# Small fp32 products of a two-layer kernel regrouped by array halves and column groups, bias rows made in one product at the head, other room for scan parameters

## The chip, the cores and the metric

One core of a Trainium2 chip runs the program. The number is the device time of one execution in microseconds; lower is better. TensorE (PE) has a granted clock of 1.2 or 2.4 GHz; the profile gives it as a share of the higher level.

## The reference

`x` is 1024 tokens by 1024 channels, fp32, and passes through two layers.

```python
# layer 1
h = rmsnorm(x, norm_mix_pre);  q, k, v, u, g_attn, g_ssm = split(h @ w_in)
# attention, 8 heads of 64 on 2 key/value heads, blocks of 128 queries on the block's own and the previous 128 keys
logits = q @ k.T / 8 + rel_bias[bucket(qpos - kpos)]          # masked to a window of 128
m = max(logits, sink);  p = exp(logits - m);  probs = p / (sum(p) + exp(sink - m))
y_attn = (probs @ v) @ w_attn_branch
# scan: 32 groups of 16 channels, one complex diagonal state of 64 each
s_t = a * s_(t-1) + B u_t;  y_t = Re(C s_t) + d_skip * u_t;  z = gelu(y);  z = z * sigmoid(z @ w_glu)
merged = sigmoid(g_attn) * y_attn + sigmoid(g_ssm) * (z @ w_ssm_branch)
x = x + rmsnorm(merged @ w_out);  x = x + rmsnorm(relu(rmsnorm(x) @ w_ff_in)**2 @ w_ff_out)
# layer 2: a gated, a convolution and a pooling branch on one big projection, and a last rmsnorm (not touched)
```

## The kernel before

The big products split each fp32 operand into a high and a low fp16 part and add three products (L208, L209, L210 in `pair_products`), and Strassen's scheme makes seven products of half size out of eight. One such product moves 512 columns. The weights come by SyncE DMAs into `raw`, a pool of three 512 KB buffers (`load_k`, L145), are subtracted on DVE (`tw`, L164) and split by ACT (`whi`, L135) and DVE (`wlo`, L136). The small products are made in fp32, which takes two passes, so two records, for each product; a transpose takes one.

The program is a list of units (`do`); each may have a `prepare` part that loads and splits its weights ahead. A scheduler then sets the order in which each engine's instructions stand, and an engine runs its own in that order; semaphores hold one until what it needs is there. So in the trace the small products of attention and scan stand between big products of other units.

**The head (L529 to L541).** Eight tiles of 128 tokens, t0 to t7, are loaded by SP. For each, ACT sums the squares (L540), POOL takes the power -0.5 (L428), DVE scales the tile (L541), PE transposes it (L448), and ACT and DVE split it. `first_pair` makes keys and values (L383): tokens 0 to 255 need t0 and t1, tokens 256 to 511 t2 and t3, the second half t4 to t7. The first queries follow in the same way.

**The bias (L573 to L592)** comes after the second half of the queries. The 32 by 8 table is copied to 128 columns for each head; eight products of 33x128x384 (L586) with a one-hot table give `vrow`, the same row in all 128 partitions; ACT copies each (L587); POOL's queue writes it to DRAM (`bdr`, L589) and reads it back so that each partition starts one element further left (`bias_t`, L591).

**Attention (L763 to L820).** `attend(n)` makes the logits of block n (L773) and the probabilities; `values(n)` transposes these (L800) and multiplies with `vtok` (L807): for each key/value head, each parity of the query head and each half of the band one product of 256 columns, that is eight in a block and four in the first. The output takes 64 of the 128 columns of the array.

**The scan (L882 to L986)** runs in four groups of eight channel groups. `ssm_tables` makes tables on DVE, 32 records of `pwk` (L921, 64 rows by 16 columns, on either half of the rows) and transposes (L934). `ssm_scan` makes `S` (L944, 32 records that alternate between the two halves of the array's columns), scans on DVE, and sums `py` from one product of `Kt` (L969, all 128 rows) and two of `CA` (L971, 64 rows) for each of eight output pieces, the three in a row.

Of the kernel before, what the change touches and what calls it, by code (L numbers as in the profile page):

```python
# [50 lines left out]
def kernel(ctx: ExitStack, tc: tile.TileContext, I: dict, out: bass.AP):  # L51
# [14 lines left out]
    def A32(kb, n):  # L66
        o = int(kb * KB) // 4
        return arena[:, o:o + n]
# [266 lines left out]
    def linear2(W, c0, act, cb, scale, early=None):  # L335
# [3 lines left out]
        def prepare():  # L339
            raw = load_k(W, lambda w: w.rearrange("(k p) n -> p k n", p=P), c0)  # L340
# [185 lines left out]
    K32 = [A32(92 + 8 * q, 4 * H).rearrange("p (k t) -> p k t", k=4) for q in range(4)]  # L526

    @do
    def _():  # L529
        xin = [A32((72, 56)[t // 4] + 4 * (t % 4), D) for t in range(NT)]  # L530
        for t in range(NT):
# [3 lines left out]
            if t == 1:  # L535
                prepare(1)
# [22 lines left out]
    bias_t = A32(84, 8 * 256).rearrange("p (h s) -> p h s", h=8)  # L559
    sink = small([P, 8], "sink")  # L560

    @do
    def _():
        nc.vector.tensor_copy(kk[0:64, 1, :], kk[64:128, 0, :])
# [7 lines left out]

    @do  # L573
    def _():

        relb = small([33, 8], "relb")
        nc.vector.memset(relb, 1.0)
        nc.gpsimd.dma_start(out=relb[0:32, :], in_=I["rel_bias"])
        hot = A32(92, 384)[0:33, :]
        nc.gpsimd.dma_start(out=hot, in_=I["onehot"])  # L580
        relrep = A32(94, 8 * P)[0:33, :].rearrange("p (h m) -> p h m", h=8)
        nc.vector.tensor_copy(relrep, relb.unsqueeze(2).to_broadcast([33, 8, P]))
        vrow = A32(108, 8 * 384).rearrange("p (h i) -> p h i", h=8)
# [6 lines left out]
        skew = bass.AP(bdr.tensor, bdr.offset + 127, [[8 * 384 - 1, P], [384, 8], [1, 256]])  # L590
        nc.gpsimd.dma_start(out=bias_t, in_=skew)  # L591
        nc.gpsimd.dma_start(out=sink, in_=I["sinks"][0].partition_broadcast(P))  # L592
# [13 lines left out]
    toff = [92.0]  # L606

    def tmp(n):
        a = A32(toff[0], n)
        toff[0] += n * 4 / KB  # L610
        assert toff[0] <= 108
        return a
# [13 lines left out]
    def _():  # L626
        L16 = tmp(3 * P)[0:16, :].rearrange("p (i m) -> p i m", i=3)
# [8 lines left out]
        prm = tmp(48).rearrange("p (i r) -> p i r", i=3)  # L636
# [3 lines left out]
        def EXP(dst, src, n):  # L640
            save = toff[0]
# [15 lines left out]
        def SINCOS(sn, cs, y, n):  # L657
            save = toff[0]
# [34 lines left out]

        dt_ = small([P, 16], "dt")
# [13 lines left out]
        TT(Ai[:, 1, :], mags[:, 0, :], snd[:, 0, :], ALU.mult)  # L708
        for m in (1, 2, 4):
# [4 lines left out]
        nr, den, f_r, f_i, t1 = (tmp(16) for _ in range(5))  # L714
# [13 lines left out]
        braw = tmp(512).rearrange("p (i r c) -> p i r c", i=2, r=NP)  # L728
# [4 lines left out]
        tb1 = tmp(256).rearrange("p (r c) -> p r c", r=NP)  # L733
        tb2 = tmp(256).rearrange("p (r c) -> p r c", r=NP)
        cmul(Bf[:, 0], Bf[:, 1], frb, fib, braw[:, 0], braw[:, 1], tb1, tb2)
        for i, n_ in enumerate(("c_re", "c_im")):
            craw = tmp(256).rearrange("p (u q) -> p u q", u=4)
# [52 lines left out]
    def values(n):  # L790
        pr = Pb[n % 2]
        for kv in range(2):
            pv = aux("pvo")
            for par in range(2):
                pt = aux("pt")
                for i in range(2):
                    h = kv * 4 + par + 2 * i
                    for half in range(2):
                        if n or half:
# [726 lines left out]
```

## Time and profile before

| what | value |
|---|---|
| median of 3 runs | 2028.05 us (2022.07 to 2031.63) |
| profiled execution | 2025.8 us, of which the span 2024.1 |
| PE busy | 1971.5 us, 97% |
| DVE busy | 1534.5 us, 76% |
| ACT busy | 875.8 us, 43% |
| POOL busy | 105.4 us, 5% |
| mean granted clock of PE | 0.994 |

The span runs from the first to the last instruction; 1.7 us of the execution lie around it. The shares are means over very different stretches: the loading of x (0 to 37 us), the first projections (to 98), attention beside big products (to about 270), the scan beside the attention gate (288 to 440) and then the rest, which the diff does not touch.

### The profile page before, as it was taken

The numbers are of one execution on the slowest core, as the hardware profiler recorded it, in microseconds if no ns is written. First come the engines' busy times: TensorE is split into PE (matmuls) and PEld (weight loads), VectorE is DVE, ScalarE is ACT, GpSimd is POOL, SyncE is SP. The second block draws the span as 40 slices with busy tenths as digits, with TensorE's granted clock in tenths as the row PEclk, the third lists the DMA queues.
The fourth block names the chain that finished last, engine by engine and source line by source line (L and its number), as shares of the span: only waits on it lengthen the run. The fifth ranks groups of instructions, "written<-read, shape, count | busy, mean of one in ns | idle before, by whom it ended". The sixth has DMA issues, their size and how long they took to land. (4 is left out here: it accounts for less than half of the span.)

```text
span 2024.1 us, 25660 instructions
## 1 busy us (share of the span) xinstructions
PE 1971.5 (97%) x9536; PEld 938.3 (46%) x9536; DVE 1534.5 (76%) x2830; ACT 875.8 (43%) x1691; POOL 105.4 (5%) x157
## 2 busy tenths in 40 slices
PE   7999999999999999999999999999999999999998
PEld 5434445554454444444444444454444443444443
DVE  7687679877568966878876578589678896899942
ACT  7316643334246735625527445434333332344511
POOL 1000000110010000000000011000000011110000
PEclk9999999999999999999999999999999999999999
DMA  5231162577321221121122422211111121112222
GB/s 182 87 109 53 42 132 69 162 235 254 104 89 63 63 73 42 63 62 53 58 68 94 126 76 86 67 43 60 63 56 62 53 63 31 63 63 68 89 84 84
DMA packets 130574, 171.80 MB, mean 85 GB/s; under 512 B 12025, under 2 KB 98293, under 8 KB 130320
## 3 DMA queue, kind: packets, MB, share of 16 engines
q1 hardware_dynamic: 124736, 160.46, 24.4%
q0 software_dynamic: 3536, 8.64, 2.4%
q10 hardware_dynamic: 2176, 1.05, 0.3%
q8 instruction: 75, 1.23, 0.2%
q14 instruction: 51, 0.42, 0.1%
HBM read 138.01 MB, written 30.93 MB: 83 GB/s over the span
## 5 line engine op out<-in xcount | busy, mean ns | idle before, releaser
L208 PE MATMUL b<-arena,whi 128*128 128x512 f16 x2044 | 776.8, 380 | 9.1 <-ACT p L226 6.5
L209 PE MATMUL b<-arena,whi 128*128 128x512 f16 x2044 | 777.2, 380 | 0.9 <-DVE arena L136 0.9
L210 PE MATMUL b<-arena,wlo 128*128 128x512 f16 x2044 | 776.5, 380 | 0.0
L135 ACT ACTIVATE whi<-tw 128x512 f16<-128x512 f32 x292 | 172.9, 622 | 337.6 <-DVE tw L164 286.8
L209 PEld LDWEIGHTS <-whi 128*128 128x128 f16 x2044 | 200.5, 98 | 253.1 <-issue 19.8
L210 PEld LDWEIGHTS <-wlo 128*128 128x128 f16 x2044 | 200.5, 98 | 243.1 <-issue 7.6
L208 PEld LDWEIGHTS <-whi 128*128 128x128 f16 x2044 | 200.5, 98 | 242.6 <-issue 8.0
L253 DVE SCALAR_TENSOR_TENSOR c<-b,u 128x512 f32<-128x512 f32 x204 | 139.7, 686 | 109.9 <-PE b L210 109.6
L136 DVE SCALAR_TENSOR_TENSOR wlo<-tw,whi 128x512 f16<-128x512 f32 x292 | 194.2, 683 | 7.7 <-ACT whi L135 7.4
L136 DVE SCALAR_TENSOR_TENSOR wlo<-raw,whi 128x512 f16<-128x512 f32 (+1 forms) x261 | 176.7, 687 | 13.9 <-ACT whi L135 13.7
L415 PEld LDWEIGHTS <-arena 128*128 128x128 f16 x1152 | 112.7, 98 | 133.2
L135 ACT ACTIVATE whi<-raw 128x512 f16<-128x512 f32 (+1 forms) x261 | 151.2, 609 | 41.5 <-PE b L209 17.0
L164 DVE TENSOR_TENSOR tw<-raw,tw 128x512 f32<-128x512 f32 x134 | 91.8, 685 | 1.4 <-DMA raw<-in_w_in_dram 0.4
L843 ACT ACTIVATE c<-c 128x512 f32<-128x512 f32 x60 | 37.7, 629 | 116.6 <-DVE c L253 98.4
L354 PE MATMUL pl<-arena,whi 128*128 128x512 f16 x320 | 83.1, 379 | 2.2 <-DVE fetch L997 1.8
L415 PE MATMUL po<-arena 128*128 128x512 f16 x384 | 84.0, 379 | 0.0
L415 PE MATMUL pf<-arena 128*128 128x512 f16 x384 | 84.0, 379 | 0.0
L415 PE MATMUL pw<-arena 128*128 128x512 f16 x384 | 83.0, 379 | 0.0
L231 DVE SCALAR_TENSOR_TENSOR u<-b,p 128x512 f32<-128x512 f32 x79 | 54.0, 684 | 33.0 <-PE b L210 32.9
L383 PE MATMUL pq<-arena,whi 128*128 128x512 f16 (+1 forms) x288 | 79.0, 360 | 0.0
L237 DVE SCALAR_TENSOR_TENSOR u<-b,u 128x512 f32<-128x512 f32 x79 | 54.1, 685 | 17.6 <-PE b L210 17.5
L226 ACT ACTIVATE p<-b 128x512 f32<-128x512 f32 x79 | 46.0, 583 | 38.2 <-PE b L210 38.2
(326 smaller groups left out, 2175.5 us busy)
## 6 DMA issues: line engine op xcount, KB each, us to landing
raw<-in_w_in_dram SPq DMA_DIRECT2D x86, 512.0 KB, 3.5
raw<-in_w_ff_in_dram SPq DMA_DIRECT2D x32, 512.0 KB, 3.6
raw<-in_w_ff_out_dram SPq DMA_DIRECT2D x32, 512.0 KB, 3.5
fetch<-gdr SPq DMA_DIRECT2D x32, 256.0 KB, 4.2
xr<-xdr SPq DMA_DIRECT2D x32, 256.0 KB, 3.4
gdr<-c SPq DMA_DIRECT2D x24, 256.0 KB, 2.0
arena<-in_x_dram SPq DMA_DIRECT2D x8, 512.0 KB, 9.9
raw<-in_w_out_dram SPq DMA_DIRECT2D x8, 512.0 KB, 5.6
```

What stands on the lines that cost most here:

```text
L135: ACT(hi, src, AF.Copy, scale=scale)
L136: STT(lo, src, scale, hi, ALU.mult, ALU.subtract)
L164: TT(t, a, b, ALU.subtract)
L208: MM(b[:, 0:n], whi[:, k], act[0][:, i, k, sl], start=(first and k == 0), stop=False, skip_group_check=not first)
L209: MM(b[:, 0:n], whi[:, k], act[1][:, i, k, sl], start=False, stop=False, skip_group_check=not first)
L210: MM(b[:, 0:n], wlo[:, k], act[0][:, i, k, sl], start=False, stop=(k == nk - 1), skip_group_check=not first)
L231: STT(v["u2"], o2, scale, v["p1"], ALU.mult, ALU.add)
L237: STT(v["u3"], o, scale, v["u2"], ALU.mult, ALU.add)
L253: STT(d, vw(o), scale, vw(v[u]), ALU.mult, ALU.add)
L354: MM(bs[s], w[:, k], a[:, k, s * H:(s + 1) * H], start=(k == 0 and w is hi and a is act[0]), stop=(k == 3 and w is lo))
L383: MM(o, w[:, k % 4], a, start=(k == 0 and w is hi and a is ahi), stop=(k == 7 and w is lo))
L415: MM(bs[s], part(a), w[:, s * H:(s + 1) * H], start=(k == 0 and a is ahi and w is whi), stop=(k == nk - 1 and a is alo))
```

## The change

- **Bias.** `bias_rows` runs while x is being loaded: one product of 33x8x384 gives the eight rows in eight partitions, ACT copies them once, and POOL's queue writes each 128 times to `bdr` (1536 KB out of 12 KB in eight partitions). `bias_read` reads it back as before, now from the unit after the first projections.
- **values.** A block has four transposes into each of four banks and four products of 512 columns, which alternate between the two halves of the array's columns; one split instead of two. The order of rows in `at` is another, so `w_attn_branch` is loaded by two DMAs of 64 partitions each (`by_kv`).
- **pwk.** The four pieces r lie in four groups of 32 columns of the array instead of side by side in the bank; four ACT copies of 16x128 stand where one of 16x512 did.
- **py.** All eight `Kt` products come first, then the sixteen `CA` products, alternating between the two halves of the array's rows and two banks.
- **Scan parameters.** Their scratch room moves from 92..108 KB, which the probabilities use later, to 131..136 and 142 onwards.

```diff
-    def linear2(W, c0, act, cb, scale, early=None):
+    def linear2(W, c0, act, cb, scale, early=None, by_kv=False):
...
+            if by_kv:
+                raw = pw.tile([P, 4, 256], F32, tag="raw", name=nm("raw"), bufs=3)
+                for a in range(2):
+                    nc.sync.dma_start(out=raw[64 * a:64 * a + 64],
+                                      in_=W[256 * a:256 * a + 256].rearrange("(k p) n -> p k n", p=64)[:, :, c0:c0 + 256])
...
+    def bias_rows():
+        relb = small([33, 8], "relb")
+        nc.vector.memset(relb, 1.0)
+        nc.gpsimd.dma_start(out=relb[0:32, :], in_=I["rel_bias"])
+        hot, row = q2("hot"), q2("vrow")
+        nc.gpsimd.dma_start(out=hot[0:33, 0:384], in_=I["onehot"])
+        pb = aux("pbias")
+        MM(pb[0:8, 0:384], relb, hot[0:33, 0:384], start=True, stop=True)
+        nc.scalar.copy(row[0:8, 0:384], pb[0:8, 0:384])
+        nc.gpsimd.dma_start(out=bdr.rearrange("p (h i) -> h p i", h=8),
+                            in_=row[0:8, 0:384].unsqueeze(1).to_broadcast([8, P, 384]))
+        nc.gpsimd.dma_start(out=sink, in_=I["sinks"][0].partition_broadcast(P))
+
+    def bias_read():
+        skew = bass.AP(bdr.tensor, bdr.offset + 127, [[8 * 384 - 1, P], [384, 8], [1, 256]])
+        nc.gpsimd.dma_start(out=bias_t, in_=skew)
...
             if t == 1:
+                bias_rows()
                 prepare(1)
...
     @do
     def _():
+        bias_read()
         nc.vector.tensor_copy(kk[0:64, 1, :], kk[64:128, 0, :])
...
-        for h in range(8):
-            pb = aux("pbias")
-            MM(pb[:, 0:384], relrep[:, h, :], hot, start=True, stop=True)
-            nc.scalar.copy(vrow[:, h, :], pb[:, 0:384])
-        bdr = pdr.tile([P, 8 * 384], F32, tag="bdr", name="bdr")
-        nc.gpsimd.dma_start(out=bdr, in_=vrow.rearrange("p h i -> p (h i)"))
...
-    toff = [92.0]
+    toff = [131.0]
...
-                for half in range(2):
-                    if n or half:
-                        MM(pv[par * 64:(par + 1) * 64, 0:256], vtok[:, n - 1 + half, kv * 64:(kv + 1) * 64],
-                           pts[:, half * 256:half * 256 + 256], start=(half == 0 or n == 0), stop=(half == 1))
...
+        parts = [(half, kv) for half in range(0 if n else 1, 2) for kv in range(2)]
+        pts = {}
+        for half, kv in parts:
+            pt = aux("pt")
+            for i in range(4):
+                nc.tensor.transpose(pt[:, i * P:(i + 1) * P], pr[:, 4 * kv + i, half * P:(half + 1) * P], ident)
+            pts[half, kv] = A32(142 + 2 * (2 * half + kv), H)
+            nc.scalar.copy(pts[half, kv], pt)
+        pv = aux("pvo")
+        for half, kv in reversed(parts):
+            MM(pv[kv * 64:(kv + 1) * 64, :], vtok[:, n - 1 + half, kv * 64:(kv + 1) * 64], pts[half, kv],
+               start=(half == 1), stop=(half == parts[0][0]))
...
+            for i in range(2):
+                for r in range(4):
+                    MM(pk[32 * r:32 * r + C, 0:P], Bf[rows, i, p0 + r, :],
+                       CA[rows, i, r, 0:8, :].rearrange("p d c -> p (d c)"), start=(i == 0), stop=(i == 1))
             for r in range(4):
-                for i in range(2):
-                    MM(pk[0:C, r * P:(r + 1) * P], Bf[rows, i, p0 + r, :],
-                       CA[rows, i, r, 0:8, :].rearrange("p d c -> p (d c)"), start=(i == 0), stop=(i == 1))
-            nc.scalar.copy(Wsb[:, :, a, :], pk[0:C, :].rearrange("p (r m) -> p r m", r=4))
+                nc.scalar.copy(Wsb[:, r, a, :], pk[32 * r:32 * r + C, 0:P])
...
+        for r in range(4):
+            for a in range(2):
+                MM(pys[a][:, cols_[r]], Kt[:, 2 * r + a, :], U[:, 2 * r + a, :], start=(r == 0), stop=False,
+                   skip_group_check=(r > 0))
+        for r in range(4):
+            for i in range(2):
+                for a in range(2):
+                    rows = slice(a * 64, (a + 1) * 64)
+                    MM(pys[a][:, cols_[r]], CA[rows, i, r, 1:9, :].rearrange("p d c -> p (d c)"), Ht[rows, i, r, :],
+                       start=False, stop=(i == 1), skip_group_check=(r > 0))
```

The scheduler gives the head another order, too. On DVE, where L541 (before) and L572 (after) scale a tile and `rs_28` (before) and `rs_32` (after) belong to t2, the rows of before are:

```order
L136 SCALAR_TENSOR_TENSOR arena<-tr_123,arena 128x4x128 [waits Activation_49]
L136 SCALAR_TENSOR_TENSOR arena<-tr_128,arena 128x4x128 [waits Activation_49]
L541 SCALAR_TENSOR_TENSOR arena<-arena,rs_24_141 128x1024 [waits DMAHW2_49,Pool_49]
L426 TENSOR_SCALAR rs_28_163<-ss_27_161 128x1 [waits DVE_49,Activation_49]
L541 SCALAR_TENSOR_TENSOR arena<-arena,rs_28_163 128x1024 [waits DMAHW5_49,Pool_49]
L136 SCALAR_TENSOR_TENSOR arena<-tr_145,arena 128x4x128 [waits Activation_49]
L136 SCALAR_TENSOR_TENSOR arena<-tr_150,arena 128x4x128 [waits Activation_49]
L426 TENSOR_SCALAR rs_32_185<-ss_31_183 128x1 [waits DVE_49]
L541 SCALAR_TENSOR_TENSOR arena<-arena,rs_32_185 128x1024 [waits DMAHW6_49,Pool_49]
```

t2 stands directly behind t1. In the changed kernel the last of the rows ahead of t2 are these (`raw_479`, `raw_648` and `raw_650` are the fourth to sixth weight loads behind those of keys and values):

```order
L136 SCALAR_TENSOR_TENSOR wlo_494<-tw_485,whi_493 128x512 [waits Activation_49]
L136 SCALAR_TENSOR_TENSOR wlo_500<-tw_497,whi_499 128x512 [waits Activation_49]
L136 SCALAR_TENSOR_TENSOR wlo_504<-raw_479,whi_503 128x512 [waits Activation_49]
L136 SCALAR_TENSOR_TENSOR wlo_510<-tw_507,whi_509 128x512 [waits Activation_49]
L136 SCALAR_TENSOR_TENSOR wlo_514<-raw_479,whi_513 128x512 [waits Activation_49]
L164 TENSOR_TENSOR tw_656<-raw_648 128x512 [waits DMAHW7_49]
L164 TENSOR_TENSOR tw_658<-raw_650,tw_656 128x512 [waits DMAHW0_49,DVE_49]
L164 TENSOR_TENSOR tw_668<-raw_650,raw_648 128x512
L164 TENSOR_TENSOR tw_678<-raw_650,tw_658 128x512 [waits DVE_49]
L572 SCALAR_TENSOR_TENSOR arena<-arena,rs_32_175 128x1024 [waits Pool_49]
L434 TENSOR_SCALAR rs_36_197<-ss_35_195 128x1 [waits DVE_49]
L572 SCALAR_TENSOR_TENSOR arena<-arena,rs_36_197 128x1024 [waits Pool_49]
```

In all 11 splits (L136) and 8 differences (L164) of six weight loads have moved ahead of t2; before, they stood behind the tiles. POOL, which issues the bias DMAs and takes the powers of the tiles, has before:

```order
L428 TENSOR_TENSOR rs_20_119<-rs_20_119,mhalf_75 128x1 [waits DVE_49]
L578 DMA relb_773<-in_rel_bias_dram 32x8
L631 DMA ldt_808<-in_log_dt_dram 16x2
L428 TENSOR_TENSOR rs_24_141<-rs_24_141,mhalf_75 128x1 [waits DVE_49,Pool_49]
L428 TENSOR_TENSOR rs_28_163<-rs_28_163,mhalf_75 128x1 [waits DVE_49,Pool_49]
L428 TENSOR_TENSOR rs_32_185<-rs_32_185,mhalf_75 128x1 [waits DVE_49,Pool_49]
L428 TENSOR_TENSOR rs_36_207<-rs_36_207,mhalf_75 128x1 [waits DVE_49,Pool_49]
L428 TENSOR_TENSOR rs_40_229<-rs_40_229,mhalf_75 128x1 [waits DVE_49,Pool_49]
L428 TENSOR_TENSOR rs_44_251<-rs_44_251,mhalf_75 128x1 [waits DVE_49,Pool_49]
L428 TENSOR_TENSOR rs_48_273<-rs_48_273,mhalf_75 128x1 [waits DVE_49,Pool_49]
L746 DMA arena<-in_d_skip_dram 16x512 [waits DMAHW1_49,DVE_49]
L580 DMA arena<-in_onehot_dram 33x384 [waits DVE_49,Activation_49]
```

And in the changed kernel:

```order
L436 TENSOR_TENSOR rs_24_131<-rs_24_131,mhalf_75 128x1 [waits DVE_49]
L641 DMA ldt_788<-in_log_dt_dram 16x2
L436 TENSOR_TENSOR rs_28_153<-rs_28_153,mhalf_75 128x1 [waits DVE_49,Pool_49]
L549 DMA bdr<-vrow_96 8x128x384 [waits Activation_49]
L436 TENSOR_TENSOR rs_32_175<-rs_32_175,mhalf_75 128x1 [waits DVE_49,Pool_49]
L436 TENSOR_TENSOR rs_36_197<-rs_36_197,mhalf_75 128x1 [waits DVE_49,Pool_49]
L556 DMA arena<-bdr 128x8x256 [waits DMASW4_49,DMAHW6_49,DVE_49,Activation_49]
L436 TENSOR_TENSOR rs_40_219<-rs_40_219,mhalf_75 128x1 [waits DVE_49,Pool_49]
L436 TENSOR_TENSOR rs_44_241<-rs_44_241,mhalf_75 128x1 [waits DVE_49,Pool_49]
L436 TENSOR_TENSOR rs_48_263<-rs_48_263,mhalf_75 128x1 [waits DVE_49,Pool_49]
L436 TENSOR_TENSOR rs_52_285<-rs_52_285,mhalf_75 128x1 [waits DVE_49,Pool_49]
L638 DMA arena<-in_lam_re_dram 16x128 [waits DMAHW1_49,DVE_49]
```

The write of `bdr` (L549) now stands ahead of t2's power, and the read (L556), which waits for the write (DMASW4), ahead of the powers of t4 to t7.

## Rows read from the trace of the kernel before

**Rows 1.** The page, busy time of the whole span (share, instructions), PE.

```profile
PE 1971.5 (97%) x9536; PEld 938.3 (46%) x9536; DVE 1534.5 (76%) x2830; ACT 875.8 (43%) x1691; POOL 105.4 (5%) x157
```

**Rows 2.** Windows: length, busy us of each engine, PEclk, DMA share, GB/s.

```profile
86.00:98.00 12.00, 12.00 (x35) 5.50 (x34) 1.50 (x3) 4.91 (x10) 1.59 (x3) 0.72 0.41 158
150.00:270.00 120.00, 119.25 (x572) 58.47 (x571) 78.94 (x279) 70.53 (x215) 5.00 (x8) 1.00 0.29 57
288.00:440.00 152.00, 150.42 (x904) 86.61 (x903) 129.43 (x242) 56.19 (x92) 19.92 (x38) 1.00 0.50 147
```

**Rows 3.** Timeline of PE, attention: start us, us, engine, line, tiles, count.

```profile
163.40 0.38 PE L208 MATMUL b<-arena,whi 128*128 128x512 f16 x1
163.71 0.65 PE L807 MATMUL pvo<-arena 128*64 128x256 f32 x2
164.29 0.66 PE L800 MATMUL pt<-ident,arena 128*128 128x128 f32 x4
...
183.11 1.08 PE L807 MATMUL pvo<-arena 128*64 128x256 f32 x4
184.12 1.13 PE L773 MATMUL lg<-arena 64*128 64x256 f32 x6
```

**Rows 4.** Timeline of PE, scan: pwk alone, and S on alternating column halves.

```profile
288.29 3.24 PE L921 MATMUL pwk<-arena 64*16 64x128 f32 x32
291.47 1.09 PE L934 MATMUL pg<-ident,arena 128*128 128x128 f32 x8
...
303.72 1.97 PE L944 MATMUL S<-arena 128*64 128x128 f32 x32
```

**Rows 5.** Timeline of PE, scan: py of one group, first rows and end.

```profile
315.99 0.38 PE L969 MATMUL py<-arena 128*128 128x128 f32 x2
316.30 1.07 PE L971 MATMUL py<-arena 64*128 64x128 f32 x4
...
324.70 0.39 PE L209 MATMUL b<-arena,whi 128*128 128x512 f16 x1
```

**Rows 6.** Timeline of PE: bias products, and the tenth big product behind them.

```profile
85.99 6.93 PE L586 MATMUL pbias<-arena 33*128 33x384 f32 x16
...
96.63 0.38 PE L208 MATMUL b<-arena,whi 128*128 128x512 f16 x1
```

**Rows 7.** Waits of DVE, 288 to 440 us: total us, times, longest.

```profile
DVE wlo L136 <- ACT whi L135: 7.3, 4, 4.2
DVE arena L949 <- PE S L944: 6.7, 4, 2.1
```

**Rows 8.** Timeline, head: DVE, ACT and PE.

```profile
9.98 1.29 DVE L136 SCALAR_TENSOR_TENSOR wlo<-raw,whi 128x512 f16<-128x512 f32 x2 [2.12 <-ACT whi L135]
...
14.82 1.07 ACT L540 ACTIVATE arena<-arena 128x1024 f32<-128x1024 f32 x1
...
16.15 1.28 DVE L541 SCALAR_TENSOR_TENSOR arena<-arena,rs 128x1024 f32<-128x1024 f32 x1 [0.73 <-POOL rs L428]
...
32.06 1.28 DVE L541 SCALAR_TENSOR_TENSOR arena<-arena,rs 128x1024 f32<-128x1024 f32 x1 [0.73 <-POOL rs L428]
```

**Rows 9.** Timeline of PE, head: first product of the second half of keys.

```profile
35.81 0.59 PE L383 MATMUL pq<-arena,whi 128*128 128x512 f16 x2
```

**Rows 10.** DMA, 0 to 40 us: busy share in 40 slices, tenths.

```profile
DMA  0459999999999999999999100000000000110396
```

**Rows 11.** DMA issues, whole run: count, KB each, median us to landing.

```profile
raw<-in_w_in_dram SPq DMA_DIRECT2D x86, 512.0 KB, 3.5
...
bdr<-arena POOLq DMA_DIRECT2D x1, 1536.0 KB, 5.4
```

**Rows 12.** DMA, 248 to 262 us: queues (packets, MB, share), then issues.

```profile
q0 software_dynamic: 399, 1.31, 87.5%
q1 hardware_dynamic: 42, 0.04, 3.9%
...
raw<-in_w_in_dram SPq DMA_DIRECT2D x1, 512.0 KB, 21.3
```

More of the change, by code (lines that the diff above doesn't have):

```diff
@@ L526 @@
     K32 = [A32(92 + 8 * q, 4 * H).rearrange("p (k t) -> p k t", k=4) for q in range(4)]
+    bias_t = A32(84, 8 * 256).rearrange("p (h s) -> p h s", h=8)
+    sink = small([P, 8], "sink")
+    bdr = pdr.tile([P, 8 * 384], F32, tag="bdr", name="bdr")
+    def bias_rows():
[13 more added lines that the diff above has]
+        nc.gpsimd.dma_start(out=bias_t, in_=skew)
     @do
@@ L605, with tmp @@
     mags = small([P, 2, 16], "mags")
-    toff = [92.0]
-    def tmp(n):
+    toff = [131.0]
+    def tmp(n, kb=None):
+        if kb is not None:
+            return A32(kb, n)
         a = A32(toff[0], n)
         toff[0] += n * 4 / KB
-        assert toff[0] <= 108
+        assert toff[0] <= 136
         return a
@@ L640, in EXP @@
         def EXP(dst, src, n):
-            save = toff[0]
+            save, toff[0] = toff[0], 131.0
             xc, t, k, r, p = (tmp(n) for _ in range(5))
@@ L692, in SINCOS @@
             toff[0] = save
+        toff[0] = 135.0
         dt_ = small([P, 16], "dt")
@@ L708, in _ @@
         TT(Ai[:, 1, :], mags[:, 0, :], snd[:, 0, :], ALU.mult)
+        toff[0] = 131.0
         for m in (1, 2, 4):
@@ L713, in _ @@
                  Ar[:, m:m + 1, :].to_broadcast([P, m, 16]), Ai[:, m:m + 1, :].to_broadcast([P, m, 16]), t1, t2)
-        nr, den, f_r, f_i, t1 = (tmp(16) for _ in range(5))
+        toff[0] = 135.75
+        nr, den, f_r, f_i = (tmp(16) for _ in range(4))
+        t1 = tmp(16, 131)
         TS(nr, Ar[:, 1, :], -1.0, None, ALU.add)
@@ L791, in values @@
         pr = Pb[n % 2]
[L792 to L795, printed above, removed]
[L796 to L810 removed]
+        parts = [(half, kv) for half in range(0 if n else 1, 2) for kv in range(2)]
[10 more added lines that the diff above has]
+               start=(half == 1), stop=(half == parts[0][0]))
+        sl = (slice(None), slice(None), slice(n * P, (n + 1) * P))
+        split(at[0][sl], at[1][sl], v4(pv), SA)
     @do
@@ L963, in ssm_scan @@
         pys = [aux("py") for _ in range(2)]
-        for a in range(2):
-            rows = slice(a * 64, (a + 1) * 64)
-            for r in range(4):
-                g = 2 * r + a
-                o = pys[a][:, r * P:(r + 1) * P]
-                MM(o, Kt[:, g, :], U[:, g, :], start=True, stop=False)
-                for i in range(2):
-                    MM(o, CA[rows, i, r, 1:9, :].rearrange("p d c -> p (d c)"), Ht[rows, i, r, :],
-                       start=False, stop=(i == 1))
+        cols_ = [slice(r * P, (r + 1) * P) for r in range(4)]
+        for r in range(4):
[8 more added lines that the diff above has]
+                       start=False, stop=(i == 1), skip_group_check=(r > 0))
+        for a in range(2):
             ACT(U.rearrange("p (r a) n -> p a r n", a=2)[:, a], pys[a].rearrange("p (r n) -> p r n", r=4),
```

44 lines of the change are left out of this document (10 added, 34 removed).

## Prediction

> **What bounds the kernel now.** I read the page first: PE is busy for 97% of the span [rows 1], so time goes where PE's work goes, unless PE starts to wait. Then windows by stage: from 150 to 270 us PE has 0.75 us of idle time and DVE 41, but from 288 to 440 us, beside the scan, DVE has only 22.6 us to spare out of 152 [rows 2]. There a gain on PE soon meets DVE. Last the timeline of each small product and of the head, where PE is fed tile by tile.
>
> The sum is made against the profiled execution, 2025.8 us, of which 1.7 lie around the span. The median of the runs, 2028.05, is 2.25 us above it; I add that at the end.
>
> **values.** A group with one product of 256 columns lasts 0.58 us from its start to the next instruction, one with two 1.01 [rows 3]: 0.43 for each product and 0.15 for getting in. Before the group the big product keeps the engine 0.31 us instead of its usual 0.21 (two of them overlap to 0.59 where one takes 0.38 [rows 9]), so 0.10 more. A group of two costs 1.11 and one of one 0.68. There are 28 and 4 of these: 33.8 us. In the changed kernel a block has four products of 512 columns, 0.86 each by the row, in one group: 0.25 + 3.44 = 3.69 if each waits for the last. But they alternate between column halves, and `S` shows what that does: its 32 records on alternating halves take 1.97 us where the 32 of `pwk`, with as many columns, take 3.24 [rows 4]; without the 0.15 at the start that is 0.59 of the time. So 0.25 + 3.44 x 0.59 = 2.28 in seven blocks and 0.25 + 1.72 x 0.59 = 1.26 in the first, 17.2 us. Gain 16.6 us; 6.0 if nothing runs side by side (7 x 3.69 + 1.97 = 27.8).
>
> **pwk.** A group lasts 3.18 us (to 291.47 [rows 4]); there are four. At `S`'s rate it would take 1.91 and the gain is 4 x 1.3 = 5 us; if four column groups overlap as well as two do twice over, 0.15 + 3.09 x 0.30 = 1.1 us, and the gain 8.3. I take 7; nothing is the other end. The 24 added ACT copies cost nothing on PE while ACT stands at 56 of 152 us [rows 2]; were that cover gone, DVE's wait for them would grow.
>
> Here the Trainium skill has a rule, in TensorEngine Tiling (Array Packing), Key Properties: different tiles of the array can load weights and multiply in parallel. By it four column groups would give the 8.3 and the sum below would be 1.3 us lower. The trace shows two halves at 0.59, not 0.5, so I stay at 7.
>
> **py.** A group lasts from 315.99 to 324.70, 8.71 us, for 48 records of 128 columns, four groups in all. These would fill 48 x 0.097 = 4.6 us at `pwk`'s rate (3.09 / 32); the rest goes with the sixteen changes between products of 128 and of 64 rows, of which the first shows 0.31 for two records and 1.00 for four [rows 5]. Now there is one such change. 16 records of `Kt` take 1.55; 32 of `CA` on alternating row halves 3.09 x 0.59 = 1.82, by `S`'s ratio; with 0.4 for getting in and the change, 3.8. Gain 4 x 4.9, less 1 since two of the groups are cut by other products: 19 us. Without overlap of row halves (3.09 for 1.82) it is 14.
>
> **Bias.** From 85.99 to 96.63 PE gets through the bias products and nine big ones, 10.64 us [rows 6], where the nine are worth 1.9. The granted clock of that window is 0.72 [rows 2]: PE fell from 2.4 to 1.2 GHz during the bias products of 33 rows and came back some way into the big ones. All of the other 8.7 us goes. The one product that is left stands at the head, before the first tile is there.
>
> PE's work falls by 16.6 + 7 + 19 + 8.7 = 51.3 us.
>
> **What comes back in attention and scan.** Between 288 and 440 us 26 us of PE's work go, so 126 are left, while DVE's busy 129.4 stay: at least 3 us come back. DVE also waits there 7.3 us for ACT's splits and 6.7 us for `S` [rows 7], which the change does not shorten. With both DVE needs 143.4 us, and 17 of the 26 come back. I take 14, near the second since both waits stand in DVE's order. From 150 to 270 us DVE has room; I take 3, between 0 and 6. Together 17; net gain 34 us.
>
> **The head.** On DVE, 19 splits and differences now stand ahead of t2's scaling. Two splits take 1.29 us [rows 8], so 19 are 12 us, but they also need their loads. There are three `raw` buffers: the fourth load waits until the first of the six is split, the sixth until the fourth has landed and been subtracted. The DMA engines are full until 22 us [rows 10], so the first is there at about 20, split at 21.5; the fourth, 3.5 us long [rows 11], lands at 25; the sixth goes out at 26.3, lands at 30, and by then DVE is in the fourth's splits until 31.5. Three more differences end at 33.5, and t2 starts at 34 instead of 16.15 [rows 8]. From t2 to t7 took 15.9 us; with no weight work between them I count 12 to 13, so t7 starts at 46 to 47 instead of 32.06, and the second half of the keys, which starts at 35.81 [rows 9] and from which PE ran without a gap, is 15 us late. The 48 products of t0 and t1 that PE can do early don't help, since t7 is late. This is the head's cost if the bias write disturbs nothing.
>
> The write can. ACT's copy of the row stands behind the square of t2, which ends at 15.9 [rows 8], so L549 goes out at about 16. How long it lasts no row shows. From 128 partitions the same 1536 KB took 5.4 us [rows 11], the lower end. The upper end comes from the reads of `udr`, 256 KB into 16 partitions each: POOL's queue moved 1.31 MB in the 14 us of that window and held the DMA engines for 87.5% of it [rows 12], 94 GB/s. If the number of partitions sets that rate, eight give half of it, and 1.57 MB take 33 us. I take this end, since that row is the nearest in shape: few partitions, one queue, engines full. The write lands at about 48.
>
> In the same window a `raw` load took 21.3 us instead of 3.5, and its queue got 3.9% of the engines. If that repeats, the fourth load, out at 21.5, lands at 49, the sixth at 54; t2 starts at 55.5, t7 at 68, and the head is 36 us late. POOL meanwhile stands at L556, but the powers behind it are needed later than that.
>
> Sum: 2025.8 - 51.3 + 17 + 36 = 2027.5 us, with 2.25 for the median 2029.8. I forecast 2030: a large gain in the middle, eaten at the head.
>
> **Rivals.**
>
> *The write is slow, but loads pass it.* In the head many loads of SP ran at once while the engines were full [rows 10], and none of them stood still as in [rows 12]. Then t2 starts at 34, but t4's power waits behind L556 until the write has landed: t4 at 49, t7 at 57, the head 25 late. 2030 - 11 = 2019.
>
> *The write is quick.* The reads of `udr` come in pieces of 512 bytes and the write goes out in pieces of 1536; if pieces and not partitions set the rate, it runs at three times 94 GB/s, takes about 6 us and lands at 22. The head is 15 late: 2030 - 21 = 2009. Against it: the engines were full at 94 GB/s, though most of what stood in their queues had far larger packets (1.31 MB in 399 [rows 12]).
>
> This is also where a rule speaks against the change. The Trainium skill, SBUF — State Buffer, Door 1: The DMA port swizzle, says that a transfer's rate depends on how many of 16 ports its partitions reach, about 27 GB/s each. Sixteen adjoining partitions reach four, eight reach two; an estimate from that page is 54 GB/s or 29 us for the write, and the sum by it would be some 4 us lower than mine. For sixteen it gives 104, which the trace's 94 roughly bears out; of a write from eight no run here shows anything.
>
> *Slower: the small products do not run side by side.* `S` alternates column halves in one bank, and no row shows four column groups, or row halves in long runs with 128 columns. If the gain is only the groups that vanish, PE gets 6 + 0 + 14 + 8.7 = 28.7; with less to gain beside the scan some 6 come back. With the head 36 late: 2025.8 - 28.7 + 6 + 36 + 2.25 = 2041. From four gains of 32 us together downwards it is slower by more than 0.5%.
>
> **Chances.** A measurement of this kernel can tell about 0.5%, 10 us, from no change: under 2018 is faster, over 2038 slower. The forecast 0.52, with a range of its own from 2021 to 2040 (write between 29 and 33 us, between 3 and 24 coming back); loads that pass 0.18; quick write 0.14; no side by side 0.16. Faster: the quick write, half of the loads that pass and a little of the forecast, 0.26. Slower: most of the last and the forecast's upper tail, 0.21. Same: 0.53. The range from 2010 to 2043 leaves out the lower half of the quick write and the far side of the slow one.
>
> **What would show it.** In the changed profile: L549 lands at 45 to 50 us, the fourth to sixth weight loads take over 15 us each or start late, t2's L572 starts after 50, and PE has 30 us or more of idle time before the second half of the keys. `values` shows L817 in seven groups of about 2.2 us, `pwk` 1 to 2 us, `py` 3.8. The granted clock stays at 1.00 around 90 us. DVE is over 90% busy beside the scan, and PE waits there for `S` or `pwk` on DVE. I am wrong if t2 starts before 40, or if L817 takes 3.6 us for four products.

## The result and the profile after

The changed kernel takes 2041.86 us in the median of four runs (2040.02 to 2044.15); the kernel before took 2027.64 beside it. The ratio is 1.0073, with an interval from 1.0057 to 1.0088: it is slower by 0.7%, 11.9 us above the forecast, and 1 us inside the upper end of the range. The profiled execution took 2041.49 us, 2039.8 of it the span.

The first number to look at is where the second half of the keys begins, since the head ends there. Timeline of PE after, from the start of the long wait (start, us, engine, line, tiles, count, idle before):

```profile
24.38 0.27 PE L391 MATMUL pq<-arena,wlo 128*128 128x256 f16 x1
...
60.48 1.94 PE L456 MATMUL tr<-ident,arena 128*128 128x128 f32 x8 [35.83 <-DVE arena L572]
...
77.50 1.24 PE L391 MATMUL pq<-arena,whi 128*128 128x512 f16 x5
```

It began at 35.81 [rows 9] and begins now at 77.50, 41.7 us later, after one wait of 35.83 us. From there to the end the changed kernel takes 1962.3 us, the kernel before 1988.3: 26.0 less. So +41.7 and -26.0 make the +15.7 between the two spans.

The cause of the wait is in the timelines of POOL and DVE after, and in its DMA issues from 14 to 50 us (count, KB each, median us to landing):

```profile
14.71 1.15 POOL L549 DMA_DIRECT2D bdr<-vrow  x1
...
60.66 0.55 POOL L436 TENSOR_TENSOR rs<-rs,mhalf 128x1 f32<-128x1 f32 x1 [42.65 <-DVE rs L434]
```

```profile
14.75 1.28 DVE L572 SCALAR_TENSOR_TENSOR arena<-arena,rs 128x1024 f32<-128x1024 f32 x1 [0.76 <-POOL rs L436]
...
43.47 1.29 DVE L136 SCALAR_TENSOR_TENSOR wlo<-raw,whi 128x512 f16<-128x512 f32 x2 [20.78 <-ACT whi L135]
...
59.06 1.28 DVE L572 SCALAR_TENSOR_TENSOR arena<-arena,rs 128x1024 f32<-128x1024 f32 x1
...
73.24 1.28 DVE L572 SCALAR_TENSOR_TENSOR arena<-arena,rs 128x1024 f32<-128x1024 f32 x1 [0.73 <-POOL rs L436]
```

```profile
raw<-in_w_in_dram SPq DMA_DIRECT2D x3, 512.0 KB, 28.3
bdr<-vrow POOLq DMA_DIRECT2D x1, 1536.0 KB, 34.2
```

The write goes out at 14.71 and takes 34.2 us. Three weight loads beside it take 28.3 in the median instead of 3.5 [rows 11]. Even loads issued before it are held: the one at 11.55 takes 31.2, the one at 13.95 takes 35.7. DVE's splits wait for the loads, t2 stands behind the splits and is scaled at 59.06 (16.15 before [rows 8]), t7 at 73.24. The queues from 24 to 48 us (packets, MB, share of the DMA engines) show the like of [rows 12], though the engines have room, with 56.4% taken in all:

```profile
q0 software_dynamic: 265, 1.19, 46.1%
q1 hardware_dynamic: 793, 0.80, 10.3%
```

The products that were regrouped do what was wanted. Timeline of PE after, a block of values, a group of pwk and one of py:

```profile
190.12 1.94 PE L817 MATMUL pvo<-arena 128*64 128x512 f32 x8
191.99 1.13 PE L787 MATMUL lg<-arena 64*128 64x256 f32 x6
...
314.29 0.68 PE L931 MATMUL pwk<-arena 64*16 64x128 f32 x32
314.90 1.09 PE L945 MATMUL pg<-ident,arena 128*128 128x128 f32 x8
...
332.43 1.95 PE L978 MATMUL py<-arena 128*128 128x128 f32 x16
334.31 2.06 PE L984 MATMUL py<-arena 64*128 64x128 f32 x32
336.30 0.39 PE L209 MATMUL b<-arena,whi 128*128 128x512 f16 x1
```

From start to next start, a block of values takes 1.87 us, 32 records of pwk 0.61 (3.18 before [rows 4]), 48 of py 3.87 (8.71 [rows 5]). PE's busy time in these lines after (us in all, mean ns of one, idle time before them and what ended it):

```profile
L817 PE MATMUL pvo<-arena 128*64 128x512 f32 x60 | 14.8, 610 | 0.7 <-ACT arena L814 0.5
L984 PE MATMUL py<-arena 64*128 64x128 f32 x128 | 8.8, 281 | 3.2 <-DVE arena L627 1.6 <-DVE arena L633 1.6
L931 PE MATMUL pwk<-arena 64*16 64x128 f32 x128 | 3.3, 273 | 8.5 <-DVE arena L627 8.4
```

Before, the same lines held 32.8 us for values, 23.0 and 15.2 for py, 12.8 for pwk and 6.9 for the bias. With py's other line, 7.8 now, and the bias product now in the head, 56.0 us of busy time leave the stretch behind the head. Only 26.0 us of time are gained there. The other 30 are in the windows (length, busy us of each engine, PEclk, DMA share, GB/s):

```profile
24.00:60.00 36.00, 0.65 (x6) 0.34 (x4) 11.51 (x18) 5.01 (x9) 0.00 (x0) 0.54 0.53 104
...
77.50:2039.80 1962.30, 1910.21 (x9298) 891.73 (x9295) 1499.90 (x2747) 840.15 (x1635) 94.10 (x134) 0.99 0.27 81
...
164.00:180.00 16.00, 14.33 (x36) 5.56 (x34) 11.45 (x60) 6.37 (x26) 0.00 (x0) 0.50 0.04 16
...
84.00:96.00 12.00, 12.00 (x57) 5.46 (x56) 11.92 (x8) 7.09 (x9) 0.00 (x0) 1.00 0.15 45
140.00:290.00 150.00, 142.45 (x652) 67.47 (x650) 119.26 (x415) 76.06 (x217) 7.70 (x11) 0.94 0.33 76
290.00:480.00 190.00, 173.05 (x1107) 87.98 (x1106) 156.21 (x277) 74.80 (x137) 21.10 (x40) 0.97 0.54 161
```

The kernel before, from 35.81 on, had 1949.54 us of PE busy in 1988.29. So busy falls by 39.3, not 56.0: other work on PE is 16.7 us longer. And idle time rises by 13.3, from 38.75 to 52.09. The last row above, from 290 to 480 us, has the scan, with 17.0 us of idle time; the same stage before, from 270 to 460, had 1.6 (188.42 of 190 busy). The row ahead of it has attention, with 7.6; before, from 90 to 270, it was 5.7 (174.33 of 180 busy). So nearly all of the new idle time is the scan's. A good part of the 16.7 is the clock. In windows of 8 us, the length times what the granted clock lacks of 1.00 adds up behind the head to some 21.7 us after and 11.4 before. The largest piece is from 164 to 180 us, at 1.2 GHz where [rows 2] show 1.00 beside attention. What PE did before it fell (timeline of PE after):

```profile
155.58 0.38 PE L208 MATMUL b<-arena,whi 128*128 128x512 f16 x1 [1.61 <-DVE u L231]
...
161.56 0.70 PE L787 MATMUL lg<-arena 64*128 64x256 f32 x2 [1.17 <-DVE m L789]
162.18 0.39 PE L210 MATMUL b<-arena,wlo 128*128 128x512 f16 x1
...
163.47 0.63 PE L209 MATMUL b<-arena,whi 128*128 128x512 f16 x1
```

There are two waits of 1.61 and 1.17 us for DVE among small products, and then a big product that starts at 163.47 takes 0.63 instead of 0.38. The start of attention had such waits before, too, and longer ones, without a fall; the last part comes back to that. From 84 to 96 us, where before the bias products cost the clock, it now stays at 1.00.

### The profile page after: what moved, and what is told of

Its sections match the earlier page's. It is cut to its first block, busy times and chain, and to the rows that moved or that the text cites. A ratio compares the mean times of both kernels' runs of the same rounds, so it can differ in the third digit from the quotient of the medians.

```text
span 2039.8 us, 25496 instructions
## 1 busy us (share of the span) xinstructions
PE 1935.9 (95%) x9462; PEld 911.6 (45%) x9462; DVE 1534.7 (75%) x2821; ACT 874.9 (43%) x1698; POOL 105.2 (5%) x157
## 3 DMA queue, kind: packets, MB, share of 16 engines
q1 hardware_dynamic: 124800, 160.46, 24.4%
## 5 line engine op out<-in xcount | busy, mean ns | idle before, releaser
L136 DVE SCALAR_TENSOR_TENSOR wlo<-tw,whi 128x512 f16<-128x512 f32 x292 | 193.8, 682 | 9.9 <-ACT whi L135 9.6
L136 DVE SCALAR_TENSOR_TENSOR wlo<-raw,whi 128x512 f16<-128x512 f32 (+1 forms) x261 | 176.2, 685 | 32.9 <-ACT whi L135 32.9
L164 DVE TENSOR_TENSOR tw<-raw,tw 128x512 f32<-128x512 f32 x134 | 91.7, 685 | 1.2
L442 ACT ACTIVATE hn<-xr 128x512 f32<-128x512 f32 x32 | 19.9, 622 | 90.4 <-issue 40.1
```

Source lines behind the costliest of these rows:

```text
L136: STT(lo, src, scale, hi, ALU.mult, ALU.subtract)
L164: TT(t, a, b, ALU.subtract)
```

## The experiments

Each ratio is to the kernel before, run on the same chip beside it (median 2030 to 2031 us).

### The bias apart from the rest

The first takes the changed kernel and gives the bias its old code and place; the second takes the kernel before and gives it the new bias alone.

```diff
# first, on the changed kernel
-                bias_rows()
...
-        bias_read()
+        for h in range(8):
+            MM(pb[:, 0:384], relrep[:, h, :], hot, start=True, stop=True)
...
+        nc.gpsimd.dma_start(out=bdr, in_=vrow.rearrange("p h i -> p (h i)"))
# second, on the kernel before: the same with - and + exchanged
```

> The changed kernel with the bias made and written as in the kernel before (eight products late, write from 128 partitions); values, pwk, py and the scan's room stay changed. Theory 'head': all of the loss is the head, where the second half of the keys starts at 77.5 us instead of 35.8. Here it starts at 36 again; behind it the changed kernel was 26 us shorter, of which 8.7 were the bias products, so 17 remain: 2011 us (2003 to 2016). Rival 'middle': the regrouped products give back what they gain to DVE's waits and to a lower clock; then 2022 to 2030.

> The kernel before with the bias at the head alone (one product, write from eight partitions), nothing regrouped. Theory 'head': t2 is scaled at about 59 us, keys' second half at 77, less 8.7 for the bias products: 2028 + 42 - 9 = 2061 us (2055 to 2066). Rival 'middle': the head is mostly made up for later, 2035 to 2045.

Without the new bias: 2003.54 us, ratio 0.9855 [0.9832, 0.9878]; the second half of the keys starts at 36.05. The new bias alone: 2077.04, ratio 1.0222 [1.0203, 1.024]; it starts at 77.37. The two multiply to 1.0074, the ratio of the whole change. So the new bias costs 45 us and the regrouping gains 29, and within the intervals neither depends on the other. Both are larger than expected: 2003.54 lies at the low end of its range, 2077.04 is 11 us above the end of its own. From two profiles the regrouping would be worth only 20 us (span 2003.9 against 2024.1); the runs of the kernel before reach from 2022 to 2037, and its profiled one, at 2025.8, lies low. So the profiles alone place a gain to no better than some 8 us.

### The write or the order

Four kernels on the changed one: the eight rows in partitions 0, 4, ... 28 instead of 0 to 7; the making and writing of the rows behind the first projections; both; and the write alone on ACT's queue.

```diff
# rows apart
+        relw = hot[0:33, 384:416]
+        nc.vector.memset(relw, 0.0)
+        nc.vector.tensor_copy(relw.rearrange("p (h q) -> p h q", h=8)[:, :, 0], relb)
-        MM(pb[0:8, 0:384], relb, hot[0:33, 0:384], start=True, stop=True)
+        MM(pb[0:32, 0:384], relw, hot[0:33, 0:384], start=True, stop=True)
-        nc.scalar.copy(row[0:8, 0:384], pb[0:8, 0:384])
+        nc.scalar.copy(row[0:32, 0:384], pb[0:32, 0:384])
...
-                            in_=row[0:8, 0:384].unsqueeze(1).to_broadcast([8, P, 384]))
+                            in_=row[0:32:4, 0:384].unsqueeze(1).to_broadcast([8, P, 384]))
# later
-                bias_rows()
...
+        bias_rows()
# write on ACT's queue
-        nc.gpsimd.dma_start(out=bdr.rearrange("p (h i) -> h p i", h=8),
+        nc.scalar.dma_start(out=bdr.rearrange("p (h i) -> h p i", h=8),
```

> The changed kernel with the eight bias rows in partitions 0, 4, 8 ... 28 instead of 0 to 7 (the product has 32 output rows); the write has the same 1024 pieces of 1536 bytes from eight partitions and the order of the engines is the same. Theory 'which partitions': the write took 34.2 us since eight adjoining partitions share few ways out; apart it takes 7 to 10 us, t2 is scaled at 33 to 36 instead of 59, and the time is 2041.9 - 24 = 2018 us (2012 to 2024). Rival 'pieces or number of partitions': it takes 34 us again and the time stays at 2042.

> The changed kernel with the rows made and written in the unit behind the first projections instead of while x is loaded; write from eight partitions as before it. DVE's order has t2 behind t1 again. Theory 'head': t2 is scaled at 16 again and the 42 us are gone; the slow write holds weight loads later instead, 34 us in which PE has its own work: it costs 5 to 20 us there. 2041.9 - 42 + 12 = 2012 us (2004 to 2022). Rival 'the write alone': wherever it stands it costs its 34 us, 2034 or more.

> The kernel of e4 (rows made and written behind the first projections) with the rows in partitions 0, 4 ... 28 as in e3. Theory 'which partitions': the write takes 8 to 10 us instead of 33.2, the weight loads beside it no longer 27.8, and the 20.5 us in which PE stood for them go, with some 7 us of later waits: 2025.5 - 27 = 1998 us (1993 to 2004). Rival 'any write at this place holds the weights': 2010 or more.

> The changed kernel with only the write of the rows issued from ACT's queue instead of POOL's. In DVE's order t2 and t3 stand directly behind t1 again, ahead of the weights; the write still goes out at about 15 us from partitions 0 to 7, and the powers of t4 to t7 still stand behind the read on POOL. Theory 'order of DVE': t2 at 16, t4 at about 50 behind the read, keys' second half at 60 to 64 instead of 77.5: 2041.9 - 15 = 2027 us (2022 to 2033). Rival 'starved loads whatever the order': 2038 or more. Rival 'order is all': 2005 to 2015.

**Rows apart:** 2021.05, ratio 0.9946 [0.993, 0.9962]. The bytes, the pieces, the place and the queue are the same. DMA issues of this kernel from 14 to 40 us, and DVE's scaling of t2:

```profile
raw<-in_w_in_dram SPq DMA_DIRECT2D x5, 512.0 KB, 4.8
bdr<-vrow POOLq DMA_DIRECT2D x1, 1536.0 KB, 14.6
```

```profile
39.87 1.28 DVE L575 SCALAR_TENSOR_TENSOR arena<-arena,rs 128x1024 f32<-128x1024 f32 x1
```

The partitions set the write's time, and with it that of the loads. The time is in the range expected, but the write is slower than the 7 to 10 us expected, and t2 later than 33 to 36. Since the order of the engines is unchanged, this run also bounds the order's own share: the second half of the keys starts at 58.32, still 22.5 us late, some of it DVE's waits for loads that still share the engines with the write. The slow write is the other 19.

**Later:** 2025.52, ratio 0.9974 [0.9959, 0.9989], against 2012 expected, 3.5 us above the end of its range. t2 is back behind t1 (scaled at 17.14), but the write only moved its harm: out at 69.57, it takes 33.2 us, three weight loads take 27.8, and PE stands still before the next projections. Waits of 70 to 110 us in this kernel (total us, times, longest), and a window:

```profile
DVE tw L164 <- DMA raw<-in_w_in_dram: 24.4, 1, 24.4
...
PE b L208 <- DVE arena L253: 20.5, 1, 20.5
```

```profile
88.00:108.00 20.00, 2.19 (x6) 0.79 (x6) 4.74 (x8) 3.71 (x7) 0.00 (x0) 0.53 0.48 87
```

**Later and apart:** 2002.37, ratio 0.9869 [0.9841, 0.9898], as expected. The write takes 11.9 us, and of DVE's wait of 24.4 us for a weight load 3.1 are left.

**Write on ACT's queue:** 2029.27, ratio 1.0003 [0.9989, 1.0018]. The time came as expected, the way there did not. t2 is scaled at 17.06, and then this (timeline of DVE of this kernel):

```profile
17.06 1.28 DVE L572 SCALAR_TENSOR_TENSOR arena<-arena,rs 128x1024 f32<-128x1024 f32 x1 [0.73 <-POOL rs L436]
42.54 0.69 DVE L164 TENSOR_TENSOR tw<-raw 128x512 f32<-128x512 f32 x1 [24.20 <-DMA raw<-in_w_in_dram]
...
49.34 1.28 DVE L572 SCALAR_TENSOR_TENSOR arena<-arena,rs 128x1024 f32<-128x1024 f32 x1 [0.73 <-POOL rs L436]
```

DVE stands before one subtraction of a starved weight load for 24.20 us, with t3's scaling behind it. So the other order brought only one more tile ahead of the starved load. The starved load holds the head under either order, and the second half of the keys starts at 65.69.

### Where the gain of values, pwk and py goes

On the kernel before: values alone; pwk and py alone; all three without the new scratch room. On the first experiment's kernel: pwk undone. The code is that of the change.

```diff
# values alone: attend's products and by_kv as in the change
# scan alone: pwk and py as in the change
# all three: both, with toff = [92.0] kept
# pwk undone, on the kernel with the old bias
-                    MM(pk[32 * r:32 * r + C, 0:P], Bf[rows, i, p0 + r, :],
+                    MM(pk[0:C, r * P:(r + 1) * P], Bf[rows, i, p0 + r, :],
...
-                nc.scalar.copy(Wsb[:, r, a, :], pk[32 * r:32 * r + C, 0:P])
+            nc.scalar.copy(Wsb[:, :, a, :], pk[0:C, :].rearrange("p (r m) -> p r m", r=4))
```

> The kernel before with values (and the loads of w_attn_branch) changed, nothing else. PE's busy time in these products fell by 18 us in the changed kernel (32.8 to 14.8). Theory: beside attention PE is the bound and nearly all stays, 2028 - 16 = 2012 us (2008 to 2017). Rival 'clock and DVE take it back': 2020 to 2028.

> The kernel before with pwk and py changed, nothing else. PE's busy time in these falls by 31 us (51.0 to 19.9), but DVE is the next bound there: waits of PE for pwk, py and S grew from about 1 to 15 us in the changed kernel, and short stretches at half clock cost some 4. Theory: 2028 - 31 + 18 = 2015 us (2010 to 2020). Rival 'PE is the bound': 1997 to 2002. Rival 'DVE takes all': 2024 or more.

> The kernel before with values, pwk and py changed; bias and room of the scan's parameters as before. e6 (values alone) gained nothing: in its scan PE waited for DVE inside the old py, the granted clock fell to half for 17 us there, and the long py ran at that clock. Theory 'clock in the old py': with the new py values' gain shows, 2028 - 17 - 13 = 1998 us (1994 to 2004), as e1 with the new room. Rival 'room': values gains nothing without the new room, 2010 to 2016, as e7.

> e1 (bias as before, the rest changed) with pwk undone. pwk gives 9.5 us of PE's work back, but PE waits 8.4 us for DVE right before it in e1. Theory 'DVE is late there': the gain of pwk is lost in that wait, and without it the time is the same, 2001 to 2007 us. Rival 'PE is the bound': 2010 to 2014.

**Values alone:** 2029.16, ratio 0.9999 [0.9986, 1.0012]. Eighteen us of PE's work are gone and nothing is gained: a miss of 17 us. `S` starts at 278.4 instead of 303.7, and then PE of this kernel runs into the old py:

```profile
356.21 0.38 PE L973 MATMUL py<-arena 128*128 128x128 f32 x2
357.71 0.48 PE L975 MATMUL py<-arena 64*128 64x128 f32 x2 [1.11 <-DVE arena L625]
360.70 0.79 PE L975 MATMUL py<-arena 64*128 64x128 f32 x2 [2.51 <-DVE arena L631]
361.43 0.79 PE L973 MATMUL py<-arena 128*128 128x128 f32 x2
362.15 1.22 PE L975 MATMUL py<-arena 64*128 64x128 f32 x4
...
374.54 0.61 PE L208 MATMUL b<-arena,whi 128*128 128x512 f16 x1
```

```profile
360.00:376.00 16.00, 15.30 (x48) 11.06 (x49) 13.00 (x34) 4.94 (x9) 0.00 (x0) 0.50 0.44 112
```

The rows with waits of 1.11 and 2.51 us are followed by the rest of the group of py, and then big products, at 1.2 GHz. Summed as above up to 600 us, 20.5 us of clock are lost, 3.4 before. That is as much as the gain that is missing. It repeats in the main: the mean granted clock, which is on record for every run, is 0.986 over the ten runs of this kernel and 0.9925 over twenty of the kernel before beside them, an estimate of 13 us (0.0065 of 2029).

**Scan alone:** 2014.82, ratio 0.9918 [0.9891, 0.9945], as expected: 17 of the 31 us of PE's busy time arrive. **All three:** 2005.59, ratio 0.9877 [0.9855, 0.9899]. That lies between the 1998 of the theory and the 2010 and more of the rival. Values adds some 8 us to the scan's gain once py is regrouped, where alone it gave none; the two intervals overlap a little, so the 8 could be nearly nothing or twice as much. The kernel with the new room (the first experiment) is at 0.9855; the share of the new scratch room cannot be told from zero.

**pwk undone:** 2020.09, ratio 0.9944 [0.9926, 0.9963], where I expected 2007 at most, and the rival 2014. pwk is worth 18 us (0.9944 less 0.9855 of 2031), though its own records are only 9.2 us longer at the full clock (12.8 against 3.6). In this profile they are 11.7 longer. Its rows show a group at the lower clock, in the profiled execution of this kernel:

```profile
341.40 0.40 PE L930 MATMUL pwk<-arena 64*16 64x128 f32 x4 [3.02 <-DVE arena L626]
...
343.75 5.28 PE L930 MATMUL pwk<-arena 64*16 64x128 f32 x28
```

```profile
344.00:352.00 8.00, 8.00 (x39) 5.41 (x38) 5.23 (x9) 1.92 (x4) 1.75 (x4) 0.50 0.39 117
```

A wait of 3.02 us, then 28 records in 5.28 us where all 32 took 3.24 before [rows 4]. This execution, at 2026.22, was the slowest of six (2016.18 the fastest), and from 100 to 564 us it lost 8.6 us of clock more than the first experiment's. The mean clocks, 0.9867 over its six runs and 0.9895 over the other's four, leave 5.7 of that as an estimate (0.0028 of 2020); and PE has 4.2 us more idle time behind the head (56.3 against 52.1). With the 9.2 that makes 19, near the 18.

### A better place for the bias

Two more on the kernel with rows apart and later: the making, writing and reading at the old place, behind the queries; and the read alone on ACT's queue.

```diff
# old place
-        bias_rows()
-        bias_read()
+    @do
+    def _():
+        bias_rows()
+        bias_read()
# read on ACT's queue
-        nc.gpsimd.dma_start(out=bias_t, in_=skew)
+        nc.scalar.dma_start(out=bias_t, in_=skew)
```

> The changed kernel with the rows made by one product behind the second half of the queries, where the eight stood in the kernel before, and written from partitions 0, 4 ... 28. Against e1 (2003.5 us) PE has seven products less, 6 us, and no 33-row run ahead of the big products, 2 us of half clock. Theory: the write and the read land no later than in e1, and the 8 us stay: 1996 us (1990 to 2001). Rival 'attention waits for the bias': the two DMAs set the start of attention, PE idles for what it saved: 2001 to 2008.

> e5 (one product behind the first projections, rows in partitions 0, 4 ... 28) with the read of the bias issued from ACT's queue instead of POOL's, where it stood behind loads of scan parameters until 118.8 us although the write had landed at 81, and where one parameter load stood behind it, for which PE waited 4.4 us. Theory 'POOL's queue': these waits and 2.8 us behind them go, and the stretch at half clock at the start of attention gets shorter: 1996 us (1991 to 2001). Rival 'the clock falls there anyway, and DVE's chain sets the start': as e5, 2001 to 2005.

Old place: 2009.15, ratio 0.9896 [0.9874, 0.9918]. That misses the range, and the rival's 2001 to 2008, too. POOL of this kernel issues the read only at 129.44, behind loads of the scan's tables, and PE waits 9.1 us for one of those. Read on ACT's queue: 2004.4, ratio 0.9881 [0.9861, 0.9901]. It goes out at 122.68, no sooner than on POOL's queue (118.83), and the time is that of the kernel without this edit, as the rival had it. Neither reached the 1996 expected. The best versions, 1.5 and 1.3% faster than before, are the regrouping with the old bias (0.9855) and with the new one later and apart (0.9869); these two cannot be told apart.

## Why the prediction was right and wrong

**The total: in part luck.** 2041.86 lies above the 2021 to 2040 that the forecast itself was given, and above the 2038 from which the prediction called it slower, with a chance of 0.21. It is the number of the rival without side by side, 2041, whose products did not come about. What brought it there is in the main one term, further down.

**The write and its victims: right.** Eight adjoining partitions took 34.2 us (33 forecast from [rows 12]), the loads beside it 28.3, t2 came at 59.06 (55.5), t7 at 73.24 (68). Both rivals that spared the head fell. Pieces of 1536 bytes do not set the rate, since rows apart have the same pieces and take 14.6 us. And no load passed the write; even the two that were issued before it were held, where the prediction counted from the fourth. One condition was wrong: the engines were not full, since the write took 46.1% of them and not 87.5, and the loads were starved all the same. POOL's hold at the read cost little, since t2 was late anyway: the read stands at 63.09 and the next power at 64.06.

The Trainium skill, SBUF — State Buffer, Door 1: The DMA port swizzle, makes a transfer's rate depend on which partitions it reaches. Its rule puts the kernels above in the order measured, its figures are too good: for eight adjoining rows it gives an estimate of 29 us, the runs 33.2 to 34.2; for rows four apart eight ports and an estimate of 7 us, the runs 11.9 to 14.6.

**The head: right in kind, 5.7 us short.** 36 forecast, 41.7 measured, of which t2 gives 3.6 and the run from t2 to t7 1.2 to 2.2: 14.2 us where I counted 12 to 13. The part of the order alone was put at 15 and is at most 22.5, as rows apart show.

**values, pwk, py: right.** 1.87 us for a block (2.28 forecast), 0.61 for a group of pwk (1.1 to 1.9, so below both; and its 1.1 takes 0.30 for 0.59 twice over, which is 0.35), 3.87 for py (3.8). The rival without side by side fell. Column halves bring the time down to half, row halves to two thirds (32 records from 334.31 to 336.30, 1.99 us, against 3.09), four column groups, sixteen records on either row half, to a fifth. The Trainium skill, TensorEngine Tiling (Array Packing), Key Properties, has different tiles of the array load and multiply in parallel; pwk agrees, with 0.61 against 3.18. With the bias the busy time that left is 56.0 us, 51.3 forecast.

**What comes back: the step that failed.** The prediction put 17 us, 14 beside the scan for DVE's 143.4 us of needs and 3 in attention. The profiles have 30: 13.3 of idle time and 16.7 of longer work. The idle time is what was forecast: 15.4 more beside the scan and 1.9 more in attention, with 4 less elsewhere. DVE as the next bound was right, though it is busy for 87% from 288 to 440 us (131.80 of 152), not for over 90. PE's waits beside the scan are those named, 8.4 us for pwk, 3.2 for py, 1.4 for `S`. The step that failed is the longer work, for which the sum had no term. By the profiles 10.3 of its 16.7 us are the clock (21.7 less 11.4): PE falls to 1.2 GHz among small products behind waits. The sum used the clock only for the bias product that it removed, never for the waits that stand or appear elsewhere. The other 6 are not traced. Against the profiled execution: -51.3 + 17 + 36 was forecast, -56.0 + 30 + 41.7 measured. That is +1.7 against +15.7, 14 us, of which 13 are this step. Values alone, which gained nothing, shows the step by itself.

A wait does not always cost the clock. The start of attention, the largest piece after, had two waits before as well, and the clock stayed. With scan alone, whose attention is that of before, nearly the same two waits end in a fall. Timeline of PE and a window, before:

```profile
135.84 0.48 PE L773 MATMUL lg<-arena 64*128 64x128 f32 x2 [2.90 <-DVE m L775]
...
141.00 0.70 PE L773 MATMUL lg<-arena 64*128 64x256 f32 x2 [1.99 <-DVE m L775]
```

```profile
140.00:144.00 4.00, 3.00 (x12) 1.29 (x12) 3.98 (x21) 0.00 (x0) 0.00 (x0) 1.00 0.02 6
```

The same of scan alone:

```profile
134.27 0.48 PE L773 MATMUL lg<-arena 64*128 64x128 f32 x2 [2.88 <-DVE m L775]
...
139.54 0.94 PE L773 MATMUL lg<-arena 64*128 64x256 f32 x2 [2.09 <-DVE m L775]
```

```profile
140.00:144.00 4.00, 4.00 (x11) 1.24 (x9) 2.84 (x17) 0.00 (x0) 0.00 (x0) 0.50 0.02 6
```

So this piece is not a price of the regrouped values, and the bias alone, with nothing regrouped, has it as well (clock 0.74 from 156 to 176 us). The waits alone do not tell when it falls due. The kernel before pays it in part, too: over 45 runs of it beside the experiments the mean clock goes from 0.990 to 0.996, and the time from 2034 us (the mean of the six runs at 0.990) to 2022 (the one at 0.996). Its profiled execution stands at 0.994, the mean of the 45 at 0.9923, an estimate of 3.4 us more lost (0.0017 of 2029). The changed kernel stands at 0.978 to 0.982, the profiled run at 0.980. So of the 10.3 us some 7 are left when runs and not profiles are compared.

By the medians what comes back can be parted. The regrouping alone takes 49.0 us out of PE's lines (83.8 before, 34.8 in the first experiment's profile) and gains 27.6 (2031.16 less 2003.54): 21 come back, where the prediction had 17. The new bias alone costs 45.9 (2077.04 less 2031.16). The head is 41.6 of it, less the 6.9 of the bias products: so 11 come back behind the head, for which the sum had nothing. In the profiles of that pair the stretch behind the head takes 1997.9 us (2075.3 less 77.37), 9.6 more than before, and there it is the clock: PE's other work is 12.0 us longer (1954.69 busy against 1949.54, without the 6.9), and the clock lost, summed as above, is 23.3 against 11.4. It falls at the start of attention and in one group of the old py, behind the waits of 1.11 and 2.51 us that values alone showed. So the larger part of the miss belongs to the late head, and the smaller to the regrouping. With the regrouping kept, every kernel in which the write was quick or out of the head was faster than before.

**Open.** Why loads are starved by a write that leaves the engines room; which waits the clock forgives; why a later head brings the waits in the old py; and the 6 us of longer work that the clock does not explain.

## What to carry to other kernels

Before a small tensor is written out many times, look at how many partitions it comes from and what loads run then: a transfer out of few adjoining partitions takes the loads beside it along, wherever it is moved, and spreading its rows costs one wider product. When PE's work shrinks or its start is late, price the waits that appear, and behind each, as a risk, the products at half the clock; a gain that leaves small products waiting can be worth nothing until those are regrouped too. Undo one part of a mixed change at a time: here a 1.5% gain and a 2.2% loss stood behind a 0.7% loss.

## What was not expected of the hardware

- The same 1536 KB out of eight partitions took 33.2 to 34.2 us from 0 to 7 and 11.9 to 14.6 from every fourth; weight loads beside them took some 28 us and 4.8 to 8.3. The slow write held only 46% of the DMA engines' time while the loads stood.
- Four column groups, sixteen records on either row half, gave 32 fp32 records of 128 columns in 0.61 us, a fifth of 3.18. Sixteen records of 128 rows and then 32 on alternating row halves took 3.87 us where the same 48 records, changing every two or four, took 8.71.
- In the stretches shown the granted clock fell to 1.2 GHz after waits of 1.1 to 3 us among small fp32 products, and stayed there for 8 to 18 us; in the kernel before, waits of 2.90 and 1.99 us among the same products left it at 2.4 GHz.
